# The last feed-forward sums four feature tiles at a time, in buffers freed by a denser layout of its right operands

## The chip, the cores and the metric

The kernel runs on one core of one Trainium2 chip. Five engines work beside each other: TensorE (PE, matmuls, with its weight loads shown as PEld), VectorE (DVE), ScalarE (ACT), GpSimd (POOL) and SyncE (SP), which issues the DMAs. The metric is the device time of one launch in microseconds (us).

## The reference, cut to what matters

The program is a two-layer trunk over 512 latent and 256 context tokens of width 1024. Each layer is a feed-forward, a token mixing (attention and a recurrent scan) and a second feed-forward. The change touches the very last feed-forward, which needs the latent tokens only, since the context is dropped after the last mixing:

```python
def swiglu(x, w_up, w_down):
    gate, up = jnp.split(x @ w_up, 2, axis=-1)
    return (jax.nn.silu(gate) * up) @ w_down
...
        x = x + 0.5 * mx[8] * swiglu(modulate(rms_norm(x, norm_gain[l, 2]), mx[6], mx[7]),
                                     ffn_up[l, 1], ffn_down[l, 1])
```

The hidden width is 2816, that is 22 feature tiles of 128.

## The kernel before, in words

Everything is float32 in value, but each operand is split into a rounded high part and a rest, and each product is three matmuls (high by high, high by rest, rest by high). Tokens lie in the free dimension: the residual stream is eight tiles `x` of 128 rows.

**Up (`up`, one call per feature tile f).** A 1 MB weight tile `raw` (`up_weights`, L339) is combined by one level of a Strassen-Winograd scheme: seven products of 12 matmuls each (tile `mw`, L365), of 258 columns in the last feed-forward (256 tokens and 2 columns for shifts). So 84 matmuls per feature. Before each product the weight is split: ScalarE makes the high part, VectorE the rest (tiles `wq`, or `whi` and `wlo`; two sums `s1` and `s2` are made by GpSimd first). VectorE adds the products up in `up_g` and `up_u`, and at the end, after the seventh product, `gated` multiplies gate and up and splits the result into the hidden tile `h2` (rows name it `h`): VectorE, ScalarE, VectorE.

**Down (`accumulate`).** After a few features their hidden tiles are multiplied by `ffn_down`. For each of 8 output tiles and 2 halves of the tokens, one PSUM bank collects 3 matmuls of 256 columns per feature (tile `mm`, L323), and one VectorE instruction (`residual`, L165, 128x256) adds the bank to `x`. The weights come in 256 KB tiles `wraw` (L310), and are split as above.

**Groups.** `FGROUPS` says how many features are summed in PSUM before the result goes to `x`: two at a time, and four in the last group. In the last feed-forward that is 9 groups of two and one of four, features 18 to 21.

**Right operands.** The seven products read 56 operand parts (7 products, 4 row tiles, high and rest) that stay put for the whole feed-forward. `prep_wino` makes them in the last down-projection of the mixing, and `operand_parts` hands out their places: it walks over buffers of the pool that are idle in a feed-forward (`PARTS`, by tag) and cuts each into pieces of `XH` = 386 columns, although the last feed-forward's parts have only 258.

**Buffers.** Tag `st` has 8 buffers of 2048 columns. `PARTS` takes three of them; the other five hold `raw` tiles and `h2` tiles. Tag `wr` has three of 512 columns, shared by `wraw`, `s1` and `s2`. `w2` and `q4` hold the split weights.

**Order.** A scheduler lays the traced program out on five engine queues by priority, when a buffer is free in its own model; each engine then runs its queue strictly in that order, and semaphores hold an instruction until its inputs and its buffer are free. All loads stand in one queue, SP's, so a load that waits for its buffer also holds the loads behind it. PSUM banks: `g` and `p` have two each and take the down sums and five of the up products; `a` and `co` take the first two up products of a feature.

Of the kernel before, what the change touches and what calls it, by code (L numbers as in the profile page):

```python
# [19 lines left out]
KD = D // 128  # L20
NF = 22
FGROUPS = tuple((f, f + 2) for f in range(0, NF - 4, 2)) + ((NF - 4, NF),)
XW = T + 2

XH = T // 2 + 2
LAT, CTX = slice(0, NL), slice(NL, T)
XLAT, XCTX = slice(0, NL), slice(NL + 2, XW)
H, HD, NP = 8, 64, 4
# [25 lines left out]
def free_ap(ap, dims, offset=0):  # L54
# [4 lines left out]
TAGS = dict(x=(2 * XH, 6), r=(2 * XH, 10), g3=(772, 3), z=(2 * XH, 3), k=(4 * XH, 2), sp=(520, 8), ob=(512, 4), ro=(256, 5),  # L59
            st=(SW, 8), w2=(512, 4), wr=(512, 3), q4=(1024, 3))  # L60


PARTS = ("st",) * 3 + ("k",) * 2 + ("sp",) * 8 + ("ob",) * 4 + ("q4",) + ("z",) * 2 + ("x",) * 6 + ("r",) * 2

BANKS = dict(g=2, ch=1, co=1, p=2, a=2)
OUTS = (0, 2, 4, 6)
# [40 lines left out]
class Net:  # L107
# [103 lines left out]
            self.stt(lo, src, scale, hi.bitcast(F32), ALU.mult, ALU.subtract)  # L211

    def prep_begin(self, l, s, ctx):
        if s != 1:
            self.raw = self.up_weights(l, s // 2, 0)
            self.parts = self.operand_parts()
        self.xh, self.xl, self.bs = {}, {}, [[] for _ in range(7)]
        self.prep_key, self.prep_ctx = (l, s), ctx

    def squares(self, kt):  # L220
        x, w = self.x[kt], T if self.prep_ctx else NL
# [8 lines left out]
    def prep(self, kt):  # L230
        if kt < 4:
            xh, xl = [self.t("r" if kt == 3 else "x", f"x{n}{kt}", XW, F32R) for n in "hl"]
        else:
            t = self.t("st", f"x2{kt}", 2 * XW, F32R)
            xh, xl = t[:, 0:XW], t[:, XW:2 * XW]
        self.xh[kt], self.xl[kt] = xh, xl
# [5 lines left out]
        self.squares(kt)  # L242

    def operand_parts(self):
        for tag in PARTS:
            t = self.t(tag, "b", dt=F32R)
            for o in range(0, TAGS[tag][0] - XH + 1, XH):
                yield t[:, o:o + XH]

    @staticmethod  # L250
    def half(ctx):
# [32 lines left out]
    def prep_end(self):  # L284
# [10 lines left out]
        nc.vector.reciprocal(rs, sd)  # L295
        self.rstd = self.t("z", "rstd", XW)
        xctx, n = (XCTX, NL) if self.prep_key[1] == 1 else (CTX, w)
# [28 lines left out]
    def project(self, src, ctx, name):  # L326
        segs = ((0, 512), (512, XW)) if ctx else ((0, 256), (256, NL + 2))
        t = self.t("g3", name, XW)
        for c0, c1, ps in self.product(self.weight(src[:, 0:4]) + self.weight(src[:, 4:8]), self.xh, self.xl, segs):
            self.tt(t[:, c0:c1], ps, self.rstd[:, c0:c1], ALU.mult)  # L330
        return t
# [74 lines left out]
    def ffn(self, l, j, ctx, after):  # L406
        s = 2 * j
        self.prep_end()
        raw = self.raw
        for f0, f1 in FGROUPS:  # L410
            hh, hl = [], []
            for f in range(f0, f1):
                now = raw
                if f + 1 < NF:
                    raw = self.up_weights(l, j, f + 1)
                h2 = self.t("st", "h2", 2 * T, F32R)
                hh.append(h2[:, 0:T])
                hl.append(h2[:, T:2 * T])
                self.up(now, ctx, hh[-1], hl[-1])
                yield  # L420
            last = f1 == NF
            yield from self.accumulate(self.a["ffn_down"][l, j], f0, f1 - f0, hh, hl, ctx, self.mods[l][:, 3 * s + 2], after if last else lambda m: None, "gp")
# [834 lines left out]
```

## Time and profile before

| | us |
|---|---|
| median of 3 timed runs (3934.7 to 3945.13) | 3942.51 |
| the profiled execution, its own time | 3928.14 |
| span of its trace | 3926.4 |
| TensorE busy in the span | 3609.1 (92%) |
| TensorE weight loads busy | 3118.2 (79%) |
| VectorE busy | 2937.6 (75%) |
| ScalarE busy | 1496.4 (38%) |
| GpSimd busy | 1004.8 (26%) |

The median is what a measurement tells; the rows below come from the one profiled execution, and times in them count from the start of its span. Its own time is 1.7 us more than the span. Shares over the span mix stages with different limits: the last feed-forward is the stretch from about 3520 to 3923 us, and that is where to look.

### The profile page before, as it was taken

The page shows a single profiled execution, that of the slowest core. Times are in us where ns is not written, and L with a number is a line of the kernel's source. Part 1 is how long each engine was busy: PE and PEld are TensorE (multiplying, and loading weights), DVE is VectorE, ACT ScalarE, POOL GpSimd, SP SyncE. Part 2 cuts the span into 40 slices and gives each one's busy share as a digit, 9 for nine tenths or more (in the row PEclk, how much of TensorE's full clock was granted, in tenths as well). Part 3 has the DMA queues.
Part 4 walks back from the last instruction along what each step waited for, and adds up shares of the span by engine and source line. Part 5 has one row for each costly group of instructions (what it writes and reads, how often), then busy time and mean ns, then how long its engine had stood idle before and what let it go on. Part 6 is the DMA issues. An engine that isn't in the chain of part 4 may idle for free. (4 is left out here: it accounts for less than half of the span.)

```text
span 3926.4 us, 73386 instructions
## 1 busy us (share of the span) xinstructions
PE 3609.1 (92%) x28980; PEld 3118.2 (79%) x28980; DVE 2937.6 (75%) x5682; ACT 1496.4 (38%) x2968; POOL 1004.8 (26%) x1156
## 2 busy tenths in 40 slices
PE   6999999999898898899999999999998987868899
PEld 4789998787565665799998999998885666758888
DVE  5678886666677765888888888886667686768888
ACT  4233334334343432533335333343433343244333
POOL 2222230202222201322233222230213132133333
PEclk7999999999798888899998999999997996889999
DMA  5421113322344253112211121223322431212222
GB/s 196 123 88 65 68 65 102 100 91 70 105 151 133 83 161 125 35 65 73 73 68 46 65 80 66 75 69 103 108 90 84 155 101 41 73 58 95 92 73 95
DMA packets 220632, 354.61 MB, mean 90 GB/s; under 512 B 46720, under 2 KB 139264, under 8 KB 208000
## 3 DMA queue, kind: packets, MB, share of 16 engines
q1 hardware_dynamic: 220288, 349.91, 27.5%
q8 instruction: 229, 3.75, 0.4%
q14 instruction: 115, 0.94, 0.1%
HBM read 306.31 MB, written 43.52 MB: 89 GB/s over the span
## 5 line engine op out<-in xcount | busy, mean ns | idle before, releaser
L365 PE MATMUL mw<-b,wq 128*128 128x386 f32 (+1 forms) x4224 | 782.6, 328 | 17.8 <-ACT wq L168 12.0
L365 PEld LDWEIGHTS mw<-b,wq 128*128 128x128 f32 x4224 | 701.8, 191 | 37.0 <-ACT wq L168 14.8
L323 PE MATMUL mm<-h,whi 128*128 128x256 f32 (+1 forms) x2816 | 661.5, 329 | 21.8 <-ACT h L168 18.0
L365 PE MATMUL mw<-b,whi 128*128 128x386 f32 (+1 forms) x2112 | 519.7, 329 | 31.8 <-ACT b L168 11.1
L323 PEld LDWEIGHTS mm<-h,whi 128*128 128x128 f32 x2816 | 474.4, 191 | 79.9 <-ACT h L168 21.5
L165 DVE SCALAR_TENSOR_TENSOR x<-mm,mods,x 128x256 f32<-128x256 f32 (+1 forms) x768 | 417.2, 573 | 155.6 <-PE mm L323 153.0
L323 PE MATMUL mm<-h,wlo 128*128 128x256 f32 (+1 forms) x1408 | 447.9, 327 | 2.0 <-DVE wlo L162 1.9
L365 PEld LDWEIGHTS mw<-b,whi 128*128 128x128 f32 x2112 | 374.3, 190 | 41.1 <-ACT b L168 14.7
L168 ACT ACTIVATE whi<-wraw 128x512 fp32r<-128x512 f32 x312 | 196.1, 629 | 491.5 <-PE mm L323 302.2
L162 DVE TENSOR_TENSOR wq<-raw,wq 128x512 fp32r<-128x512 f32 x352 | 298.6, 849 | 70.0 <-ACT wq L168 68.1
L365 PE MATMUL mw<-b,wlo 128*128 128x386 f32 (+1 forms) x1056 | 347.0, 329 | 1.1 <-DVE wlo L162 0.8
L168 ACT ACTIVATE wq<-raw 128x512 fp32r<-128x512 f32 x352 | 219.7, 628 | 326.5 <-PE mw L365 272.3
L323 PEld LDWEIGHTS mm<-h,wlo 128*128 128x128 f32 x1408 | 267.4, 191 | 27.8 <-DVE wlo L162 2.8
L162 DVE TENSOR_TENSOR wlo<-wraw,whi 128x512 fp32r<-128x512 f32 x312 | 221.2, 710 | 57.9 <-ACT whi L168 35.9
L162 DVE TENSOR_TENSOR up_g<-up_g,mw 128x386 f32<-128x386 f32 (+1 forms) x352 | 182.3, 518 | 82.3 <-PE mw L365 72.6
L162 POOL TENSOR_TENSOR raw<-raw,s 128x512 f32<-128x512 f32 x88 | 124.0, 1409 | 432.5 <-DVE wq L162 429.7
L162 POOL TENSOR_TENSOR s<-raw 128x512 f32<-128x512 f32 x88 | 126.4, 1436 | 421.5 <-DVE wlo L162 360.7
L168 ACT ACTIVATE whi<-s 128x512 fp32r<-128x512 f32 x176 | 110.4, 628 | 294.7 <-PE mm L323 206.6
L323 PE MATMUL mm<-x,whi 128*128 128x258 f32 (+2 forms) x832 | 208.3, 336 | 0.0
L365 PEld LDWEIGHTS mw<-b,wlo 128*128 128x128 f32 x1056 | 201.2, 191 | 3.2 <-DVE wlo L162 2.4
L185 PE MATMUL modps<-wmod,cs 128*32 128x256 f32 x1152 | 167.7, 439 | 34.0 <-DMA wmod<-in_w_mod_dram 33.2
L162 POOL TENSOR_TENSOR up_g<-up_g,rstd 128x386 f32<-128x386 f32 (+1 forms) x88 | 100.8, 1145 | 348.8 <-DVE up_g L162 348.8
(226 smaller groups left out, 6992.5 us busy)
## 6 DMA issues: line engine op xcount, KB each, us to landing
raw<-in_ffn_up_dram SPq DMA_DIRECT2D x88, 1024.0 KB, 5.3
wmod<-in_w_mod_dram SPq DMA_DIRECT2D x208, 256.0 KB, 2.9
wraw<-in_ffn_down_dram SPq DMA_DIRECT2D x176, 256.0 KB, 3.2
wraw<-in_w_in_dram SPq DMA_DIRECT2D x104, 256.0 KB, 2.9
wmod<-in_w_mod_dram SPq DMA_DIRECT2D x96, 128.0 KB, 2.3
wmod<-in_w_mod_dram SPq DMA_DIRECT2D x8, 1024.0 KB, 10.4
wraw<-in_w_out_dram SPq DMA_DIRECT2D x32, 256.0 KB, 3.2
in<-rkv SPq DMA_DIRECT2D x20, 384.0 KB, 3.9
```

The lines of the kernel that those rows point to most:

```text
L162: (eng or self.nc.vector).tensor_tensor(out=out, in0=a, in1=b, op=op)
L165: self.nc.vector.scalar_tensor_tensor(out=out, in0=a, scalar=s, in1=b, op0=op0, op1=op1)
L168: self.nc.scalar.activation(out, in_, f, **kw)
L185: nc.tensor.matmul(ps[q:q + 32], lhsT=self.cs[:, kt], rhs=w, start=kt == 0, stop=kt == KD - 1)
L323: nc.tensor.matmul(ps, lhsT=wt, rhs=xt[k][:, c0:c1], start=k == 0 and n == 0, stop=k == nk - 1 and n == 2)
L365: nc.tensor.matmul(ps, lhsT=wt[:, c], rhs=self.bs[i][k][xt], start=k == 0 and m == 0, stop=k == 3 and m == 2)
```

## The change: what it does

The last feed-forward gets its own table of groups, five of four features and a last one of two (features 20 and 21). To make room for four hidden tiles and the weight tiles beside them, its operand parts are cut at 258 columns, so that an `st` buffer holds seven instead of five, a `k` buffer five instead of four, an `sp` buffer two instead of one, a `q4` buffer three instead of two. The list of buffers for them takes one `st` buffer where it took three, so seven are left for `raw` and `h2`. The reordered lines of `prep_begin` only set `prep_ctx` before it is read. The other three feed-forwards keep their layout and their groups.

```diff
+FGROUPS_LAT = tuple((f, min(f + 4, NF)) for f in range(0, NF, 4))
...
+PARTS_LAT = ("st",) + PARTS[3:]
...
     def prep_begin(self, l, s, ctx):
+        self.xh, self.xl, self.bs = {}, {}, [[] for _ in range(7)]
+        self.prep_key, self.prep_ctx = (l, s), ctx
         if s != 1:
             self.raw = self.up_weights(l, s // 2, 0)
             self.parts = self.operand_parts()
-        self.xh, self.xl, self.bs = {}, {}, [[] for _ in range(7)]
-        self.prep_key, self.prep_ctx = (l, s), ctx
...
     def operand_parts(self):
-        for tag in PARTS:
+        h = self.half(self.prep_ctx)
+        for tag in PARTS if self.prep_ctx else PARTS_LAT:
             t = self.t(tag, "b", dt=F32R)
-            for o in range(0, TAGS[tag][0] - XH + 1, XH):
-                yield t[:, o:o + XH]
+            for o in range(0, TAGS[tag][0] - h + 1, h):
+                yield t[:, o:o + h]
...
-        for f0, f1 in FGROUPS:
+        for f0, f1 in FGROUPS if ctx else FGROUPS_LAT:
```

The lines below stand four lines later in the changed program (L314 for L310, L327 for L323, L369 for L365), and the scheduler lays the last feed-forward out anew on every engine.

On TensorE, before, this is the end of a group of two in the middle of the stage: `mw` rows are up products, `mm` rows are down sums, `h_36589` is the hidden tile of the group's first feature and `h_36734` that of its second.

```order
L365 MATMUL mw<-b,whi 128x258 x2
L365 MATMUL mw<-b,wlo 128x258
L323 MATMUL mm<-h_36589,whi 128x256 x2
L323 MATMUL mm<-h_36589,wlo 128x256
L323 MATMUL mm<-h_36589,whi 128x256 x2
L323 MATMUL mm<-h_36589,wlo 128x256
L365 MATMUL mw<-b,wq 128x258 x2
L323 MATMUL mm<-h_36589,whi 128x256 x2
L323 MATMUL mm<-h_36589,wlo 128x256
L365 MATMUL mw<-b,wq 128x258 x22
L323 MATMUL mm<-h_36589,whi 128x256 x2
L323 MATMUL mm<-h_36589,wlo 128x256
L323 MATMUL mm<-h_36734,whi 128x256 x5
```

Between the last matmul of the group's last up (the second row) and the first that needs its last hidden tile (the last row) stand 12 `mm` and 24 `mw` of the next feature, 36 matmuls.

After, at the end of a group of four on TensorE (`h_37373`, `h_37518` and `h_37663` are the hidden tiles of its first three features, `h_37808` that of the fourth), the last rows of the same passage are these:

```order
L327 MATMUL mm<-h_37373,wlo 128x256
L327 MATMUL mm<-h_37518,whi 128x256 x2
L327 MATMUL mm<-h_37518,wlo 128x256
L327 MATMUL mm<-h_37663,whi 128x256 x2
L327 MATMUL mm<-h_37663,wlo 128x256
L369 MATMUL mw<-b,wq 128x258 x6
L327 MATMUL mm<-h_37808,whi 128x256 x5
```

Counted from the last up matmul to the row of `h_37808`, 36 `mm` (three features in four banks) and 24 `mw` of the next feature stand between, 60 matmuls. Such an end occurs four times, and a fifth one differs in a few rows.

In SP's queue, before, one period of two features reads like this; `raw` is the 1 MB up weight of a feature, `wraw` a 256 KB down weight:

```order
L310 DMA wraw<-in_ffn_down_dram 128x2x256 x3
L339 DMA raw<-in_ffn_up_dram 128x2048
L310 DMA wraw<-in_ffn_down_dram 128x2x256
L339 DMA raw<-in_ffn_up_dram 128x2048
```

and after, one period of four features:

```order
L314 DMA wraw<-in_ffn_down_dram 128x512
L343 DMA raw<-in_ffn_up_dram 128x2048
L314 DMA wraw<-in_ffn_down_dram 128x512 x4
L343 DMA raw<-in_ffn_up_dram 128x2048
L314 DMA wraw<-in_ffn_down_dram 128x512 x3
L343 DMA raw<-in_ffn_up_dram 128x2048 x2
```

The up weight of the next group's first feature stood behind three down weights, and stands behind one; the last two of a period stand together behind all eight.

The very last group, on TensorE after, has two features (`h_39077`, `h_39220`) and nothing behind it to fill in:

```order
L327 MATMUL mm<-h_39077,whi 128x256 x2
L327 MATMUL mm<-h_39077,wlo 128x256
L327 MATMUL mm<-h_39220,whi 128x256 x5
L327 MATMUL mm<-h_39220,wlo 128x256
L327 MATMUL mm<-h_39220,whi 128x256
```

Between its last up matmul and the first that needs its last hidden tile stand 12 `mm`; before, in the last group of four, 36.

## Rows read from the trace of the kernel before

**Rows 1.** Busy time by engine in four stretches of the last feed-forward, and granted clock.

```profile
core 0: us, PE busy (x) PEld busy (x) DVE busy (x) ACT busy (x) POOL busy (x), PEclk, DMA share, GB/s
3520.20:3559.74 39.54, 36.85 (x274) 36.08 (x275) 33.68 (x70) 18.49 (x35) 13.27 (x11) 0.92 0.22 74
3559.74:3858.18 298.44, 267.37 (x2112) 261.82 (x2113) 256.10 (x497) 113.72 (x208) 107.97 (x81) 0.97 0.25 86
3858.18:3899.50 41.32, 39.16 (x316) 38.33 (x317) 39.33 (x76) 19.45 (x37) 20.02 (x13) 1.00 0.24 75
3899.50:3923.47 23.97, 23.17 (x190) 22.53 (x188) 14.47 (x30) 5.49 (x10) 0.00 (x0) 1.00 0.38 125
```

**Rows 2.** Waits of TensorE, 3559.74 to 3858.18: who for whom, us, times, longest.

```profile
PE mm L323 <- ACT h L168: 16.2, 8, 2.4
PE mw L365 <- ACT wq L168: 8.0, 7, 1.4
PE mw L365 <- DVE x L165: 3.7, 5, 0.9
PE mm L323 <- DVE h L162: 2.7, 3, 0.9
PE mw L365 <- ACT whi L168: 1.2, 2, 0.7
```

**Rows 3.** Chain of waits, 3559 to 3640: start us, us, what.

```profile
3559.74 11.30 PE mw L365 x93
3571.04 7.47 DMA raw<-in_ffn_up_dram
...
3608.20 7.47 DMA raw<-in_ffn_up_dram
```

**Rows 4.** Timeline of the DMA issues on SP, 3672 to 3690.

```profile
3673.78 9.57 SPq L310 DMA_DIRECT2D wraw<-in_ffn_down_dram  x3
3683.41 0.59 SPq L339 DMA_DIRECT2D raw<-in_ffn_up_dram  x1
```

**Rows 5.** Timeline of ScalarE (ACT), 3690 to 3693.

```profile
3691.03 1.15 ACT L168 ACTIVATE wq<-raw 128x512 fp32r<-128x512 f32 x2 [4.89 <-DMA raw<-in_ffn_up_dram]
```

**Rows 6.** Timeline of TensorE (PE), 3691.5 to 3698.5.

```profile
3691.72 0.51 PE L365 MATMUL mw<-b,wq 128*128 128x258 f32 x2 [1.38 <-ACT wq L168]
...
3698.00 0.80 PE L323 MATMUL mm<-h,whi 128*128 128x256 f32 x2 [2.43 <-ACT h L168]
```

**Rows 7.** Clock and busy time in two stretches of 10 us.

```profile
3620.00:3630.00 10.00, 7.58 (x52) 7.38 (x51) 8.38 (x16) 2.33 (x5) 5.25 (x5) 0.83 0.00 0
3690.00:3700.00 10.00, 6.19 (x42) 5.78 (x42) 7.01 (x12) 4.03 (x8) 3.64 (x3) 0.88 0.28 109
```

**Rows 8.** Chain of waits, 3858 to 3926.

```profile
3891.91 7.30 PE mw L365 x58
3899.21 4.99 PE mm L323 x42
...
3906.54 16.42 PE mm L323 x136
```

**Rows 9.** Groups of VectorE (DVE) instructions by shape, 3520.2 to 3923.47.

```profile
L165 DVE SCALAR_TENSOR_TENSOR x<-mm,mods,x 128x256 f32<-128x256 f32 x160 | 70.1, 478 | 20.1 <-PE mm L323 19.7
```

**Rows 10.** Timeline of VectorE (DVE), 3865 to 3903.

```profile
3886.95 1.18 DVE L162 TENSOR_TENSOR up_u<-up_u,rstd 128x256 f32<-128x256 f32 x1
...
3898.93 0.42 DVE L162 TENSOR_TENSOR up_u<-up_u,rstd 128x256 f32<-128x256 f32 x1
...
3901.83 0.83 DVE L162 TENSOR_TENSOR h<-up_u,h 128x254 fp32r<-128x254 f32 x2
```

**Rows 11.** DMA issues of 3520 to 3926: count, KB each, median us to landing.

```profile
raw<-in_ffn_up_dram SPq DMA_DIRECT2D x20, 1024.0 KB, 7.0
```

**Rows 12.** Chain of waits, 3440 to 3500.

```profile
3456.19 0.90 PE co L951 x14
...
3487.43 1.35 DVE b L162
```

## The prediction, made before the changed kernel ran

> **What bounds the kernel now.** Only the last feed-forward changes, so I read that stretch first by engine [rows 1]. In its middle, 298.4 us that hold eight groups of two features, TensorE is busy for 267.4 us and VectorE for 256.1 us: neither is idle for long, and neither is full. The reader should see that the stage has no single full engine, so its time must be read from waits.
>
> First the floor. In the tail of the stage 136 down matmuls follow each other without a gap in 16.42 us [rows 8], and 93 up matmuls take 11.30 us [rows 3]: 0.12 us each. A group of two has 168 up and 96 down matmuls, 264 in all, 31.7 us. Eight groups would take 253.4 us and take 298.4, so 45.0 us are lost, 5.6 per group. The waits of TensorE there [rows 2] sum to 31.8 us: 18.9 for the hidden tile of the group's last feature (16.2 for its high part on ScalarE, 2.7 for the rest on VectorE), 8.0 for a split up weight `wq`, 4.9 for a bank or a split at the end of the down sums. The mean clock was 0.97 [rows 1], worth about 9 us more; the last 4 us go in the refilling after each wait.
>
> Next, what stands behind the two big waits. The chain of waits [rows 3] runs every 37 us through an up weight's DMA: 7.47 us, then ScalarE's split. SP's timeline tells why it is late [rows 4]: three down weights, each waiting for a `wr` buffer, take from 3673.78 to 3683.35 to go out, and the up weight of the next group's first feature, queued behind them, goes out at 3683.41. ScalarE has waited 4.89 us for it when it starts its split at 3691.03 [rows 5]. TensorE waits for that split (1.38 us), and VectorE's queue, which has the same split ahead of the last feature's gating, is late too, so the hidden tile costs TensorE another 2.43 us at 3698.0 [rows 6]. Both waits have one cause, and they come at every second feature. In the 10 us around such waits the granted clock shows 0.83 and 0.88 [rows 7], against 1.00 in the ups of the last group, where TensorE runs on [rows 1].
>
> The last group of the kernel before is a group of four already, and shows what one costs: from 3858.18 to the last matmul at 3922.96 it runs 504 matmuls (24 came before) in 64.8 us, at clock 1.00. The floor is 60.5, so it loses 4.3 us. Between its last up and its first use of the last hidden tile stood 36 matmuls, and TensorE went on without a gap: the up products end at 3899.2, the down sums start in the same 0.1 us [rows 8], and the hidden tile is there at 3902.66 [rows 10].
>
> **The change part by part.** *Matmuls, weight loads and splits* keep their number: 1848 up and 1056 down matmuls, 22 up weights of 1 MB and 44 down weights of 256 KB either way. No term.
>
> *VectorE's additions to the residual* fall from 160 to 96. They take 70.1 us for 160 [rows 9], 0.44 each, so 28 us of VectorE's work go. I don't count them as time: they lie beside matmuls in the down sums, where VectorE sits idle for TensorE's `mm` (20.1 us before the 160). What they do is leave VectorE idle in the down sums, and that makes the splits of the next feature early.
>
> *Group ends.* Where two groups of two stood, a group of four keeps one boundary (after the down sums TensorE waits for a bank or split: 4.9/8 = 0.6, with refilling 0.9) and the loss of the four-feature run as measured in the tail, 4.3. Why should the waits for weight and hidden tile go? The first up weight of the next group now stands behind one down weight and not three, so it is issued about 9 us earlier (the 9.57 us of [rows 4]); it was late by 4.9. And behind the last up product there are 60 matmuls, 7.2 us, before the hidden tile is needed; it takes 3.5 us (3899.2 to 3902.66), some 5 with two more splits of 0.7 ahead of it in VectorE's queue. So the cover is about 2 us longer than the need. Lost per four features: 5.2 in place of 11.2, four times (features 4 to 19).
>
> *The run of four ups.* The 4.3 us are VectorE's: in the tail the same instruction of the last two features starts at 3886.95 and 3898.93 [rows 10], 12.0 us apart, where TensorE needs 84 x 0.12 = 10.1. VectorE is the slower one in an up phase, and catches up in the down sums. This speaks for keeping the groups small; it is in the 4.3.
>
> *The start.* The first 288 matmuls, 3520.2 to 3559.74, took 39.5 us against a floor of 34.6, 5.0 lost, at a clock of 0.92 [rows 1]; the second group lost 5.6. After, the first four features lose that start and a VectorE-bound run: 5.0 + 4.0 in place of 10.6.
>
> *The end.* The last group has two features and only 12 matmuls, 1.4 us, between its last up and the hidden tile, which takes 3.5: a new wait of 2.1 us, and if the clock drops behind it as in [rows 7], 1.7 more (0.17 of 10 us); I take 3.0. With a boundary (0.9) and 1.4 for its one VectorE-bound feature, the end loses 5.3.
>
> *The denser layout* of the 56 parts costs nothing by itself: same sizes, same instructions. It takes the scan's `k` buffers earlier in its list; the scan's last matmuls are at 3456 and the first part is written at 3487 [rows 12], 30 us later. If that cover were gone, the start would slip by as much as the buffer is late. Four up weights instead of two stand at the head of the stage, 7.0 us each [rows 11]; they are needed 10 us apart.
>
> *The transfer pair.* The third and fourth up weight of a group now go out together when the old hidden tiles are released, at the end of the down sums. The third is needed 60 + 84 matmuls later, 17.3 us. Two loads of 7.0 us [rows 11], one after the other or side by side, need 14. Hidden, with 3 us to spare.
>
> Sum: before loses 5.0 + 45.0 + 4.3 = 54.3 us of the 402.8 in which the stage runs 2904 matmuls (348.5). After: 9.0 + 4 x 5.2 + 5.3 = 35.1. Gain 19.2 us: span 3926.4 - 19.2 = 3907.2, own time 3908.9. The median of the runs shown is 0.37% above that profiled execution; 0.49% off it gives 3923.
>
> Unknown costs, from both sides: the four-feature run may lose as little as 1 us (if the slack in the down sums lets VectorE run ahead), or as much as 4 x 1.9 = 7.6 (if VectorE is never ahead). Over five runs that moves the gain by 16 us up or down. The end's wait lies between 0 and 3.8.
>
> **The rivals.**
>
> *VectorE takes the gain back (no change).* With runs of four, each feature costs 12.0 us in all of them: 7.6 in place of 4.3 per run, so five runs take back 16.5 of the 19.2 us: 3940, within what a measurement can tell. For it: VectorE was 95% busy in the tail's ups (39.33 of 41.32 us [rows 1]). Against: the tail lost 4.3 with exactly such a run, after a down sum in which VectorE had less slack than it will have.
> The Trainium skill, "Perfetto Trace Analysis", section "Identifying the Most-Contended Engine", has a rule that points here: judge TensorE by how busy its weight loads are and work on the fullest engine. In the middle stretch weight loads are busy for 261.8 of 298.4 us, VectorE for 256.1 [rows 1]; by that rule TensorE is the fullest, its work stays, and taking 28 us off VectorE gives nothing: 3942, with a chance that lies within this rival's. The trace agrees on who is fullest; the rows on waits say that 12% are left beside the weight loads, and that most of it goes in waits that the change removes.
>
> *The pair of up weights is late (slower).* If SP's queue holds the pair longer, TensorE stops at the third feature of four groups. Each us past 17.3 costs four; the gain is gone when the third weight lands 19.2/4 = 4.8 us late, 22 us after release, and at 25 us (7.8 late, 31 us in all) the kernel is slower by 0.3%, 3954. For it: the pair stands behind all eight down weights. Against: by then these have gone, as the down sums are over; 7.0 us each is what the trace shows [rows 11].
>
> *More than forecast.* VectorE ahead after each down sum: 1 to 2 us per run in place of 4.3, gain 30 to 35, about 3909.
>
> **How the numbers follow.** Forecast 0.60; gain taken back, in all or most, 0.18; slower 0.06; more 0.16. The likeliest gives 3923, its own range 3914 to 3930. The range 3905 to 3936 takes in the case of more and the nearer part of the gain taken back, with the spread of the runs shown (3934.7 to 3945.13). About 0.3%, 12 us, is also what a measurement of this kernel can tell from no change. Faster by over 0.3%: 0.76; same: 0.18; slower: 0.06.
>
> **What would show it.** Right: from the first `mw` to the last `mm` some 383 us instead of 402.8; period of a group of four 68 to 69 us where two groups took 74.6; ScalarE's wait for `raw` at a group's end under 1 us (it was 4.89); no wait of `mm` for ScalarE's `h` except one of 2 to 3 us at the very end; granted clock 0.99 or more; 28 us less on VectorE. Wrong: waits of `mw` for `wq` or `wlo` of VectorE growing past 5 us per run of four (first rival), or a wait for the DMA of `raw` at the third feature of a group (second). The forecast fails if the next group's first up weight is still late, since then both old waits stay, once per four features.

## The result, and the profile after

The changed kernel takes 3917.23 us (median of 15 runs, 3902.43 to 3937.81), the kernel before 3937.61 us beside it on the same chip (15 runs, 3929.39 to 3953.06). The ratio is 0.9946, with a 95% interval of 0.993 to 0.9962: faster by 0.54%, some 21 us.

The profiled execution has a span of 3915.4 us, 11.0 less than before. That is not the gain of the stage. The first eight `ssps` matmuls, with which the last feed-forward's ups begin, start at 3520.8 before and at 3532.6 after: what lies ahead took 11.8 us longer in this execution, and it scatters that much (e11). From there to the end of the last matmul it is 402.2 us before (to 3922.95) and 379.4 after (to 3912.04), 22.8 less. I call this length **the stage** below and judge the experiments by it. By the prediction's count, from the first `mw` at the head, it is 402.8 and 380.4.

The page of the kernel after, span and busy times:

```profile
span 3915.4 us, 73285 instructions
PE 3616.3 (92%) x28980; PEld 3121.2 (80%) x28980; DVE 2924.9 (75%) x5618; ACT 1496.0 (38%) x2968; POOL 1013.9 (26%) x1156
```

The busy times hardly differ from those of before; the gain is in waits. The windows view of the stage (us, then busy time of each engine, granted clock, DMA share, GB/s), cut at the head, at the same place of four groups of four, and at the end, answers to [rows 1]:

```profile
3531.68:3612.24 80.56, 74.67 (x542) 71.75 (x543) 64.95 (x117) 33.03 (x62) 28.03 (x21) 0.91 0.17 53
3612.24:3679.66 67.42, 64.88 (x531) 63.61 (x530) 59.52 (x109) 28.43 (x53) 29.64 (x20) 1.00 0.27 95
3679.66:3747.07 67.41, 64.89 (x530) 63.62 (x530) 59.43 (x109) 28.43 (x53) 29.64 (x20) 1.00 0.28 95
...
3881.86:3912.10 30.24, 29.29 (x240) 28.61 (x239) 26.92 (x59) 10.96 (x20) 4.10 (x3) 1.00 0.26 89
```

Four features take 67.4 us, four times over, where two groups of two took 74.6, and the granted clock in them is 1.00 (0.97 before [rows 1]). The waits of TensorE from 3612.24 to 3881.86, over four groups (line, releaser: total, times, longest), answer to [rows 2]. In the rows of the changed kernel VectorE's splits and sums stand at L165 (L162 before), ScalarE's work at L171 (L168 before), and the addition of a bank at L168 (L165 before).

```profile
PE mw L369 <- DVE wq L165: 7.3, 8, 1.3
PE mw L369 <- DVE wlo L165: 1.3, 4, 0.3
PE mm L327 <- ACT whi L171: 0.7, 4, 0.2
```

9.3 us in 269.6 where 31.8 stood in 298.4. The waits for ScalarE's `wq` and for the hidden tile `h` are gone. SP's timeline of one group says why (start, duration, line; the up weight is `raw`), against [rows 4]:

```profile
3634.69 0.33 SPq L314 DMA_DIRECT2D wraw<-in_ffn_down_dram  x1
3635.06 0.43 SPq L343 DMA_DIRECT2D raw<-in_ffn_up_dram  x1
3645.72 9.81 SPq L314 DMA_DIRECT2D wraw<-in_ffn_down_dram  x4
3655.57 0.42 SPq L343 DMA_DIRECT2D raw<-in_ffn_up_dram  x1
3663.23 4.30 SPq L314 DMA_DIRECT2D wraw<-in_ffn_down_dram  x3
3678.62 1.04 SPq L343 DMA_DIRECT2D raw<-in_ffn_up_dram  x2
```

The next group's first up weight goes out at 3635.06 behind one down weight, and TensorE enters the down sums at 3653.1; nobody waits for it. The first group is different. SP, then ScalarE, then TensorE there:

```profile
3564.83 11.54 SPq L314 DMA_DIRECT2D wraw<-in_ffn_down_dram  x3
3576.46 0.38 SPq L343 DMA_DIRECT2D raw<-in_ffn_up_dram  x1
```

```profile
3584.53 1.15 ACT L171 ACTIVATE wq<-raw 128x512 fp32r<-128x512 f32 x2 [6.33 <-DMA raw<-in_ffn_up_dram]
```

```profile
3558.75 3.99 PE L369 MATMUL mw<-b,wq 128*128 128x258 f32 x20 [2.27 <-DVE wq L165]
3585.22 1.03 PE L369 MATMUL mw<-b,wq 128*128 128x258 f32 x4 [1.38 <-ACT wq L171]
...
3901.34 1.21 PE L327 MATMUL mm<-h,whi 128*128 128x256 f32 x5 [0.80 <-ACT h L171]
```

There the up weight still stands behind three down weights, and the wait of 1.38 us is as in [rows 6]. The wait of 2.27 us, the longest of the head, comes some 18 us before that weight goes out and has another cause, which the account of the start below takes up. The granted clock over the head is 0.91. The last row is the wait at the very end, 0.80 us.

### The profile page after: what moved, and what is told of

Same layout as the page of the kernel before. It is cut to its first block, busy times and chain, and to the rows that moved or that the text cites. A ratio compares the mean times of both kernels' runs of the same rounds, so it can differ in the third digit from the quotient of the medians.

```text
span 3915.4 us, 73285 instructions
## 1 busy us (share of the span) xinstructions
PE 3616.3 (92%) x28980; PEld 3121.2 (80%) x28980; DVE 2924.9 (75%) x5618; ACT 1496.0 (38%) x2968; POOL 1013.9 (26%) x1156
## 5 line engine op out<-in xcount | busy, mean ns | idle before, releaser
L369 PE MATMUL mw<-b,wq 128*128 128x386 f32 (+1 forms) x4224 | 787.0, 329 | 19.4 <-DVE wq L165 15.1
L369 PEld LDWEIGHTS mw<-b,wq 128*128 128x128 f32 x4224 | 704.0, 191 | 39.3 <-DVE wq L165 19.3
L327 PE MATMUL mm<-h,whi 128*128 128x256 f32 (+1 forms) x2816 | 652.6, 326 | 2.6 <-ACT h L171 0.8
L369 PE MATMUL mw<-b,whi 128*128 128x386 f32 (+1 forms) x2112 | 518.4, 328 | 24.6 <-DVE b L165 11.3
L327 PEld LDWEIGHTS mm<-h,whi 128*128 128x128 f32 x2816 | 467.6, 188 | 59.6 <-issue 8.5
L168 DVE SCALAR_TENSOR_TENSOR x<-mm,mods,x 128x256 f32<-128x256 f32 (+1 forms) x704 | 390.7, 581 | 159.5 <-PE mm L327 157.1
L327 PE MATMUL mm<-h,wlo 128*128 128x256 f32 (+1 forms) x1408 | 440.6, 325 | 2.7 <-DVE wlo L165 2.3
L369 PEld LDWEIGHTS mw<-b,whi 128*128 128x128 f32 x2112 | 374.1, 191 | 32.2 <-DVE b L165 14.0
L171 ACT ACTIVATE whi<-wraw 128x512 fp32r<-128x512 f32 x312 | 195.8, 629 | 500.2 <-PE mm L327 298.3
L165 DVE TENSOR_TENSOR wq<-raw,wq 128x512 fp32r<-128x512 f32 x352 | 313.2, 892 | 52.0 <-ACT wq L171 50.1
L369 PE MATMUL mw<-b,wlo 128*128 128x386 f32 (+1 forms) x1056 | 347.0, 329 | 3.4 <-DVE wlo L165 3.0
L171 ACT ACTIVATE wq<-raw 128x512 fp32r<-128x512 f32 x352 | 220.1, 629 | 312.1 <-PE mw L369 288.8
L327 PEld LDWEIGHTS mm<-h,wlo 128*128 128x128 f32 x1408 | 261.8, 188 | 29.5 <-DVE wlo L165 4.4
L165 DVE TENSOR_TENSOR wlo<-wraw,whi 128x512 fp32r<-128x512 f32 x312 | 224.9, 723 | 57.7 <-ACT whi L171 34.3
L165 DVE TENSOR_TENSOR up_g<-up_g,mw 128x386 f32<-128x386 f32 (+1 forms) x352 | 182.0, 518 | 86.1 <-PE mw L369 77.1
L165 POOL TENSOR_TENSOR raw<-raw,s 128x512 f32<-128x512 f32 x88 | 123.8, 1407 | 407.3 <-DVE wq L165 404.8
L165 POOL TENSOR_TENSOR s<-raw 128x512 f32<-128x512 f32 x88 | 125.2, 1423 | 394.8 <-DVE wlo L165 317.3
L171 ACT ACTIVATE whi<-s 128x512 fp32r<-128x512 f32 x176 | 110.0, 628 | 281.9 <-PE mm L327 198.9
L165 POOL TENSOR_TENSOR up_g<-up_g,rstd 128x386 f32<-128x386 f32 (+1 forms) x88 | 107.5, 1221 | 405.1 <-DVE up_g L165 405.1
L327 PE MATMUL mm<-x,whi 128*128 128x258 f32 (+2 forms) x832 | 208.5, 337 | 0.0
L369 PEld LDWEIGHTS mw<-b,wlo 128*128 128x128 f32 x1056 | 201.2, 191 | 7.4 <-DVE wlo L165 6.5
```

The source lines that it names most:

```text
L165: (eng or self.nc.vector).tensor_tensor(out=out, in0=a, in1=b, op=op)
L168: self.nc.vector.scalar_tensor_tensor(out=out, in0=a, scalar=s, in1=b, op0=op0, op1=op1)
L171: self.nc.scalar.activation(out, in_, f, **kw)
L327: nc.tensor.matmul(ps, lhsT=wt, rhs=xt[k][:, c0:c1], start=k == 0 and n == 0, stop=k == nk - 1 and n == 2)
L369: nc.tensor.matmul(ps, lhsT=wt[:, c], rhs=self.bs[i][k][xt], start=k == 0 and m == 0, stop=k == 3 and m == 2)
```

## The experiments

**The same kernels again (e11, e12).** How far does the stage repeat?

> The changed kernel once more, unchanged, to see how far the length of the stage repeats from one profiled execution to another. My theory, that the stage is set by the order of the instructions and hardly by chance: 379.4 us within 1 us, periods of 67.4. Rival, that the start of the stage scatters: off by 3 us or more, and then the difference of 5.4 us with the group of two first says little.

> The kernel before once more, unchanged. My theory: stage 402.2 us within 1 us, and the 10 us and more by which spans differ lie in the mixing ahead of it. Rival: off by 3 us or more.

Measured: 377.7 us (3514.0 to 3891.7) with periods of 67.4 again, and 403.2 (3522.3 to 3925.5). The two pairs repeat to 1.7 and 1.1 us; that is a bit more than I expected, and a difference of under 2 us between two stages is not read below. The spans of the changed kernel, 3915.4 and 3895.1, differ by 20: they scatter ahead of the stage.

**The layout without the groups (e1).**

```diff
-        for f0, f1 in FGROUPS if ctx else FGROUPS_LAT:
+        for f0, f1 in FGROUPS:
```

> The denser layout and the seven st buffers stay, but the last feed-forward keeps the groups of before (nine of two, one of four). My theory, that the grouping pays because the next group's first up weight stands behind fewer down weights and more down matmuls cover the hidden tile: nothing is gained, as that up weight still stands behind three down weights in SP's queue; two groups of two take 74 to 75 us as before, ScalarE still waits 4 to 5 us for raw at a group's end, first matmul to last about 402 us. Rival, that free buffers alone bring the weights early enough: two groups take 68 to 70 us and the stage 380 to 385 us, as in the changed kernel.

Stage 404.1 us, two groups of two 73.4 to 76.8 (74.6 before), ratio to before 1.0014 (0.9993 to 1.0035). SP and ScalarE:

```profile
3592.27 9.55 SPq L314 DMA_DIRECT2D wraw<-in_ffn_down_dram  x3
3601.87 0.59 SPq L343 DMA_DIRECT2D raw<-in_ffn_up_dram  x1
```

```profile
3609.47 1.15 ACT L171 ACTIVATE wq<-raw 128x512 fp32r<-128x512 f32 x2 [4.86 <-DMA raw<-in_ffn_up_dram]
```

The same 9.55 us and the same wait of 4.86 us as in [rows 4, 5]. Room alone brings nothing.

**The groups without the layout (e2).**

```diff
     def operand_parts(self):
-        h = self.half(self.prep_ctx)
-        for tag in PARTS if self.prep_ctx else PARTS_LAT:
+        h = XH
+        for tag in PARTS:
```

> Groups of four with the old layout, so that four hidden tiles and the weights share five st buffers. My theory: the next group's first up weight is still issued early, so most of the gain stays; but the second one of a group can be issued only when an old hidden tile is released at the end of the down sums, and it is needed some 10 us later (84 matmuls) at the first product of the second feature, with a load of 7 us, a split and three loads at a time behind the release: 1 to 4 us lost per group, a period of 68.5 to 71.5 us, the stage 385 to 397 us. Rival, that the grouping is worth nothing without the room: stage 400 us or more.

Stage 388.5 us, period 69.2, ratio 0.9981 (0.9959 to 1.0003), which by itself cannot be told from no change. The stage is in between, as my theory had it: with five `st` buffers the three remaining up weights go out behind one another, within 4.9 us, at the end of the down sums.

```profile
3582.60 4.30 SPq L314 DMA_DIRECT2D wraw<-in_ffn_down_dram  x3
3598.01 4.88 SPq L343 DMA_DIRECT2D raw<-in_ffn_up_dram  x3
```

So grouping without room keeps some 14 of the 23 us of the stage; the room is worth the other 9. ScalarE waits for the first of them,

```profile
3602.82 0.63 ACT L171 ACTIVATE wq<-raw 128x512 fp32r<-128x512 f32 x1 [1.06 <-DMA raw<-in_ffn_up_dram]
```

and behind it TensorE's waits for `wq` and `wlo` of VectorE are 12.2 us in four groups, where the changed kernel has 8.6.

**Early weights, groups of two (e3 with the dense layout, e6 with the old one).** The main test: the supposed cause is cured by itself, with no group of four. Each up weight is loaded one feature earlier, in the last feed-forward only; e3 has the groups of e1, e6 is the kernel before.

```diff
-                if f + 1 < NF:
-                    raw = self.up_weights(l, j, f + 1)
+                if ctx:
+                    raw = self.up_weights(l, j, f + 1) if f + 1 < NF else None
+                else:
+                    if f == 0:
+                        nxt = [self.up_weights(l, j, 1)]
+                    if f + 2 < NF:
+                        nxt.append(self.up_weights(l, j, f + 2))
+                    raw = nxt.pop(0) if nxt else None
```

> Dense layout, groups of two as before, but each up weight of the last feed-forward is loaded one feature earlier, so that it no longer stands late in SP's queue behind the down weights of its own group's end. My theory says that one cause, the late up weight, stands behind both big waits: then the waits of TensorE for the first wq of a group and for the hidden tile nearly go, and two groups of two take 68 to 71 us in place of 74.6, with no group of four. Rival, that the 36 matmuls between the last up product and the hidden tile are too few, or VectorE's additions too many: the wait for the hidden tile stays at 1.5 to 2.5 us per group and two groups take 72 to 75 us.

> The kernel before, with its old layout, five st buffers and groups of two, and only the early load of the up weights added. A group of two holds two hidden tiles, so five st buffers leave three for up weights. My theory, that the early load needs little room with groups of two: the stage takes 379 to 386 us, nearly as with the dense layout (378.5). Rival, that without the seven st buffers the early load waits for a buffer and stands in SP's queue, so that nothing is gained: 396 to 403 us.

Stage 378.5 us (e3) and 378.0 (e6), ratios 0.9938 (0.9913 to 0.9962) and 0.9931 (0.9905 to 0.9958). The kernel before with this one edit, no new layout and no group of four gets all that the change gets. Windows of e6, two groups of two each, and the waits of TensorE in eight groups:

```profile
3572.09:3640.68 68.59, 64.40 (x529) 63.51 (x529) 64.24 (x125) 29.21 (x53) 27.24 (x21) 1.00 0.27 93
3640.68:3709.24 68.56, 64.39 (x528) 63.50 (x529) 64.21 (x125) 28.99 (x52) 27.16 (x21) 1.00 0.28 93
```

```profile
PE mm L323 <- ACT h L168: 9.8, 8, 1.2
PE mw L365 <- DVE x L165: 6.4, 8, 0.9
```

ScalarE, over the same groups, waits for no DMA of `raw` any more. Before (3559.74 to 3858.18) it had this row:

```profile
ACT wq L168 <- DMA raw<-in_ffn_up_dram: 32.6, 7, 4.9
```

Against [rows 2]: TensorE's wait for `wq` (8.0 us) is gone, and that for the hidden tile fell from 18.9 us to 9.8. So a late up weight stood behind the first wait wholly and behind half of the second. The other half, 1.2 us per group, is the short cover of 36 matmuls, as my rival had it. VectorE has all 160 additions here and is busy for 64.24 of 68.59 us, and still the period is 6.0 us shorter than before.

**Early weights, groups of four (e5).** Edit of e3 on the changed kernel.

> The changed kernel (dense layout, groups of four) and each up weight of the last feed-forward loaded one feature earlier. The late weight is now cured only in the middle groups; in the first group it still stood behind three down weights (11.54 us). My theory, that a late up weight is the cause of nearly all that was lost and that the number of VectorE's additions is worth little: the middle periods stay at 67 to 68 us, the first group gets 2 to 5 us shorter, the stage from its first sum of squares to the last matmul 374 to 378 us (379.4 in the changed kernel, 378.5 with groups of two and early weights). Rival, that grouping by four and early weights are two separate gains that add up: 20 us less than groups of two with early weights, under 365 us.

Stage 375.6 us, ratio 0.9915 (0.9885 to 0.9946), the lowest of the study, though its interval overlaps that of the change. Windows of e5, from the head to the first long down sum, and the next period:

```profile
3517.75:3574.75 57.00, 53.26 (x402) 51.15 (x402) 51.06 (x99) 28.26 (x54) 18.41 (x15) 0.94 0.23 79
3574.75:3642.58 67.83, 64.94 (x528) 63.53 (x529) 60.50 (x108) 28.54 (x52) 26.64 (x19) 1.00 0.27 94
```

The same stretch of the changed kernel:

```profile
3532.60:3595.85 63.25, 57.48 (x402) 54.85 (x403) 50.78 (x98) 28.44 (x54) 18.60 (x15) 0.89 0.16 55
```

The head is 6.3 us shorter and the periods 0.4 longer. Both the late weight and the wait of 2.27 us are gone from the head, so the 6.3 us are not the price of the late weight alone. The two gains don't add up: once the weights are on time, four features at a time bring 2.4 to 2.9 us over two (375.6 against 378.0 and 378.5), near the 1.7 to which a stage repeats.

**The VectorE additions put back (e4 on the changed kernel, e10 on e5).**

```diff
         for c0, c1, ps in product:
...
             self.stt(xs, ps, gate[:, m, j:j + 1], xs, ALU.mult, ALU.add)
+            if twice:
+                self.stt(self.t("ro", "spare", 256), ps, gate[:, m, j:j + 1], xs, ALU.mult, ALU.add)
```

> The changed kernel with 64 more VectorE additions of 128x256, 16 in each of the down sums of four groups, written to a spare buffer (the output is the same): VectorE has again as many additions as before the change. My theory, that the 28 us of VectorE count for little since it idles in the down sums: a period of four features goes from 67.4 to 68 to 70 us, the last feed-forward is 2 to 10 us longer. Rival, that the relief of VectorE is what pays: 7 us per period, about 74, and the whole gain is gone.

Stage 394.1 us, 14.7 more than the changed kernel, ratio 0.9965 (0.9941 to 0.9988): between the two theories, so at first it told nothing. Windows of e4, first a period without spare additions, then three with them; and SP and ScalarE in the third of these windows:

```profile
3594.19:3662.19 68.00, 64.19 (x522) 62.99 (x523) 60.45 (x110) 28.42 (x52) 30.22 (x21) 1.00 0.28 94
3662.19:3732.94 70.75, 67.04 (x528) 65.26 (x528) 64.42 (x125) 28.46 (x52) 28.46 (x20) 0.98 0.27 90
3732.94:3803.01 70.07, 65.77 (x528) 63.70 (x529) 64.33 (x125) 28.47 (x52) 28.95 (x21) 1.00 0.27 91
3803.01:3874.51 71.50, 67.31 (x528) 65.23 (x528) 64.43 (x125) 28.49 (x52) 28.97 (x21) 0.98 0.27 89
```

```profile
3772.71 12.63 SPq L314 DMA_DIRECT2D wraw<-in_ffn_down_dram  x3
3785.40 0.42 SPq L343 DMA_DIRECT2D raw<-in_ffn_up_dram  x1
```

```profile
3793.08 1.15 ACT L171 ACTIVATE wq<-raw 128x512 fp32r<-128x512 f32 x2 [5.71 <-DMA raw<-in_ffn_up_dram]
```

The additions changed the scheduler's order, and the up weight stood behind three down weights again. The experiment mixed two causes. With early weights it can't:

> The kernel with groups of four and early weights (stage 375.6 us, period 67.8), with the 64 spare VectorE additions of 128x256 in the down sums of four groups. In the changed kernel they cost 14.7 us, but they also brought the late up weight back (raw behind three down weights, ScalarE waiting up to 5.7 us for it). My theory, that the late weight was most of that price: with early weights the additions cost 0 to 1.5 us per period, stage 375.6 to 382 us. Rival, that VectorE's relief itself is worth 3 to 4 us per period: stage 387 to 391 us.

Stage 380.9 us, 5.3 more than e5, ratio 0.9937 (0.9916 to 0.9959), periods 69.05 to 69.20 in place of 67.83:

```profile
3661.01:3730.10 69.09, 65.54 (x528) 63.72 (x528) 65.47 (x125) 28.23 (x52) 28.61 (x20) 1.00 0.27 92
```

So 16 additions (some 7 us of VectorE) cost 1.3 us per period by themselves, and 2.7 to 4.1 with the late weight that they brought back (70.07 to 71.50 against 67.4).

**Fewer VectorE instructions in the ups (e7).** Four instructions per feature are left out in the last feed-forward, so part of the computation is missing.

```diff
-        self.tt(t1[:, b], t1[:, b], p, ALU.add)
+        if ctx:
+            self.tt(t1[:, b], t1[:, b], p, ALU.add)
...
-        self.tt(t2[:, h:e], t2[:, h:e], self.rstd[:, h:e], ALU.mult)
+        if ctx:
+            self.tt(t2[:, h:e], t2[:, h:e], self.rstd[:, h:e], ALU.mult)
```

(and likewise for the two other scalings)

> The changed kernel without four of VectorE's instructions per feature in the up products of the last feed-forward (one addition of a product and the three scalings by rstd are left out, so part of the computation is missing). They cost some 1.7 us per feature. My theory, that the 4.0 us that a group of four still loses are VectorE's in the run of four ups: the period of four features falls from 67.4 to 64.3 to 65.5 us and the waits of mw for wq and wlo go. Rival, that they come from refilling after waits and from the down sums: 67 us or more.

Stage 361.5 us, period 65.30 us:

```profile
3653.58:3718.88 65.30, 63.82 (x530) 63.40 (x530) 54.82 (x93) 28.21 (x53) 26.68 (x20) 1.00 0.29 98
```

Of the 4.0 us that a group of four loses against 528 x 0.12 = 63.4, 2.1 go with these instructions of VectorE. The scheduler also laid the down sums out in another order, so this is the price of the edit and not of the instructions alone. The rest stays, in one wait for `up_g` (1.0 us) and one for `wlo` (0.5) per group.

**The short group first (e8), and both cures (e9).**

```diff
-FGROUPS_LAT = tuple((f, min(f + 4, NF)) for f in range(0, NF, 4))
+FGROUPS_LAT = ((0, 2),) + tuple((f, f + 4) for f in range(2, NF, 4))
```

> The changed kernel with the group of two first and five groups of four behind it, where the changed kernel has it last. My theory: the end has 36 more matmuls of cover for the last hidden tile, but the measured wait there is only 0.80 us, and the last run of four loses 3 to 4 us instead of 1 to 2; the start has one late weight after a shorter run. Within 3 us of the changed kernel either way, stage 376.5 to 382.5 us. Rival, that the start is what costs and a short first group cures it: 4 us or more shorter.

> Dense layout, the group of two first, then fours, and the up weights loaded one feature earlier. With fours alone the short first group brought the stage to 374.0 us and the early weights to 375.6 (379.4 in the changed kernel), both at the start. My theory, that both cure the same late weight of the first group: together no more than either, 372 to 375 us. Rival, that they are two things: 368 to 371 us.

e8: stage 374.0 us, ratio 0.9923 (0.9896 to 0.9949); 5.4 and 3.7 us under the two executions of the changed kernel, so against my theory and by its size on the rival's side, but at its edge. e9, which adds the early weights: 376.7 us, ratio 0.9945 (0.9925 to 0.9966). Together they give no more than either. That both cure the same late weight does not follow: in e8 the up weight still goes out late in the head, behind three down weights,

```profile
3545.37 15.55 SPq L314 DMA_DIRECT2D wraw<-in_ffn_down_dram  x3
3560.95 0.60 SPq L343 DMA_DIRECT2D raw<-in_ffn_up_dram  x1
```

and ScalarE waits 2.78 us for it; only TensorE does not wait for its split. What the heads of e5 and e8 both lack is the wait of 2.27 us. That e9 came out 2.7 above e8 I can't explain (its periods are 67.9 where those of e8 are 67.4 and 67.6).

| stage, us | weights as before | weights one feature earlier |
|---|---|---|
| groups of two, old layout | 402.2, 403.2 | 378.0 |
| groups of two, dense layout | 404.1 | 378.5 |
| groups of four, old layout | 388.5 | not tried |
| groups of four, dense layout | 379.4, 377.7 | 375.6 |

The cut at `ssps` hides one thing, the start of the very first up product, before and after:

```profile
3505.71 0.48 PE L365 MATMUL mw<-b,whi 128*128 128x258 f32 x2 [0.79 <-DVE x L165]
3519.22 0.48 PE L369 MATMUL mw<-b,whi 128*128 128x258 f32 x2 [0.42 <-DVE x L168]
```

With the old layout it lies 15.1 us ahead of the first `ssps`, with the dense one 13.4, the same to 0.02 us in all executions of either layout. So beside the old layout the stage shows the dense kernels 1.7 us too long. Counted from this first `mw`, the rows of the table read 417.2, 418.3 and 393.0; 417.5 and 391.9; 403.6; 392.8, 391.1 and 389.0. The order stays: the change takes 24.4 us off, the early weights alone 24.2, the layout alone nothing, and the room in a group of four is worth 10.8 (12.5 against e11).

## Why the prediction was right, point by point

**One cause for both waits.** Shown for the wait for `wq` and for half of that for the hidden tile (18.9 us to 9.8 in e6); the other half was the short cover of 36 matmuls, so "one cause" said too much. Loading early alone, in either layout, takes 24 to 26 us off the stage. The change reached the same place by another way, since a group of four happens to leave the next up weight behind one down weight and puts 60 matmuls of cover before the hidden tile.

**The sum.** Forecast 19.2 us off 402.8; measured 22.4 (380.4). That it came within 3.2 us is partly luck: three larger errors nearly cancel. *The start* (552 matmuls, up to 3612.24) was forecast at 66.2 + 9.0 = 75.2 us and took 80.56. I took the early weight for all groups, and in the first one it stands behind three down weights, which take 11.54 us; TensorE waits 1.38 us for it. More of its waits come earlier, in the second feature: 0.56, 0.78 and 2.27 us between 3553 and 3559, and the granted clock is 0.79 around the last:

```profile
3556.00:3564.00 8.00, 5.73 (x35) 5.51 (x35) 7.17 (x15) 4.13 (x8) 2.04 (x2) 0.79 0.01 2
```

There VectorE is behind, and two of its instructions that take 0.87 us at the end of the third feature took 3.04 at the end of the first, beside GpSimd, whose three sums for the next products run from 3549.79 to 3553.95 (first and third row VectorE, second row GpSimd):

```profile
3549.77 3.04 DVE L168 SCALAR_TENSOR_TENSOR up_u<-up_u,up_g 128x254 f32<-128x254 f32 x2 [0.55 <-ACT up_g L171]
3549.79 1.28 POOL L165 TENSOR_TENSOR s<-raw 128x512 f32<-128x512 f32 x1
3576.35 0.87 DVE L168 SCALAR_TENSOR_TENSOR up_u<-up_u,up_g 128x254 f32<-128x254 f32 x2
```

The wait of 2.27 us is there again in e11 (2.25), and no wait in the head of e5 is over 1 us. That GpSimd is what makes VectorE late is not tested, and no run parts this wait from the late weight, so how the 5.4 us divide between them stays open. *The run of four with its boundary* was to lose 5.2 us and lost 4.0, four times, 4.6 less in all. The tail of before, from which I took 4.3 for the run alone, was not a typical run; why it lost more I didn't test. *The end* was to lose 5.3 and lost 1.4: the hidden tile is there 2.4 us after the last up product (3898.95 to 3901.34), not the 3.5 of [rows 8, 10], which were read behind a run of four; 0.80 us of waiting in place of 3.0.

**VectorE's additions at nothing.** Too low by a little. Their work fell from 70.1 us [rows 9] to 43.9, 26 less where 28 were forecast:

```profile
L168 DVE SCALAR_TENSOR_TENSOR x<-mm,mods,x 128x256 f32<-128x256 f32 x96 | 43.9, 479 | 23.4 <-PE mm L327 23.3
```

and e10 prices 64 of them at 5.3 us in groups of four, 0.19 us of time for each us of VectorE. I take that as an upper price, since a spare addition also holds its bank; no run tests this.

**The cover of 60 matmuls.** Right: no wait of `mm` for `h` in the middle groups. e6 shows the 36 of a group of two short by 1.2 us even with the weight on time.

**The pair of up weights.** Hidden, as forecast: no wait for a DMA of `raw` from 3612 to 3882. e2, where three go out behind one another, shows what the rival feared, at 1.8 us per period.

**The dense layout.** Costs nothing and gives nothing by itself (e1).

**VectorE takes the gain back.** No: `wq` and `wlo` of VectorE cost TensorE 8.6 us in four groups, 2.15 per run, under the 5 at which I would have given in. e7 agrees with 2.1.

The rule in the Trainium skill's "Perfetto Trace Analysis", section "Identifying the Most-Contended Engine", by which TensorE's weight loads are what to work on, would have said no change as the prediction read it. They are as busy after as before over the whole span (3121.2 us against 3118.2), while their share of the middle stretch rose from 88% [rows 1] to 94% (63.61 of 67.42): it names the floor rightly and says nothing of the 12% above it. The same page's section "Optimization Strategy" bears on this better: a gap that repeats can mean too few buffers for the next tile. Here a load does wait for a buffer, but it is not the load whose tile is missing: seven `st` buffers in place of five left the gap as it was (e1), and a `raw` that is merely queued one feature earlier, with five, took most of it away (e6).

## What to carry to other kernels

When an engine waits for a load, look at what stands ahead of it in its queue before making room for it: a load that waits for its own buffer delays all behind it, and loading a tile one step earlier was the cheaper cure here. Try that cure by itself before a larger change that happens to include it, since the two need not add up. And where a scheduler lays out the order, read the order again after every edit: 64 additions on another engine were enough to bring the late load back.

## What the runs showed of the hardware

The part ahead of the stage scatters far more than the stage: the first `ssps` lies between 3514.0 and 3551.2 us over the profiled executions, while the stage of one kernel repeats to 1.7 us (two pairs). Over whole runs of one kernel the length goes with the mean granted clock: spans of 3887.5 us at 0.938 and 3924.1 at 0.925 (e8). Inside the stage the granted clock is lower where TensorE waits more: 0.89 over the head of the changed kernel, 0.94 over that of e5, 1.00 in the middle periods of the changed kernel, 0.97 in those of before [rows 1], and 0.98 in two of e4's three periods with a late weight.

VectorE is slower beside GpSimd in some of its work. In the stage of the changed kernel its split `wlo` of a sum `s` takes 0.68 us where no GpSimd instruction runs and 1.44 where one does (medians of 16 and 26); the addition of a PSUM bank takes 0.48 and 0.47.
